# A two-direction delta-rule scan taken in lockstep over two head pairs, with its triangular inversion cut into three queued pieces

## The chip, the core and the metric

One core of one Trainium2 chip runs the whole kernel. The metric is the device time of one execution in microseconds (us), the median of three runs; lower is better.

The core has five instruction queues that run side by side and each keep their own order: TensorE (PE in the profile, with its weight loads as PEld), VectorE (DVE), ScalarE (ACT), GpSimd (POOL) and SyncE (SP, which here only issues DMAs; ACT and POOL issue some too). An instruction waits until the semaphores it needs are set, and everything behind it on its queue waits with it.

## The reference

One layer of a hybrid backbone: 1024 latent tokens and 256 context tokens, width 1024. The token mixer has three branches (neighbourhood attention, RWKV-7 time mixing, gMLP gating), then comes a SwiGLU network. The change is in the RWKV branch, a recurrence over the tokens in both directions, for 8 heads of width 64:

```python
def delta_scan(state0, inputs, emit):
    def step(S, inp):
        r_t, w_t, k_t, v_t, kk_t, a_t = inp
        s_kk = jnp.einsum('...vk,...k->...v', S, kk_t)
        S = (S * w_t[..., None, :] - s_kk[..., :, None] * (kk_t * a_t)[..., None, :]
             + v_t[..., :, None] * k_t[..., None, :])
        return S, (jnp.einsum('...vk,...k->...v', S, r_t) if emit else None)
    return lax.scan(step, state0, inputs)
...
state_ctx, ys_c = delta_scan(state0, scan_c, ctx_out)     # 256 context tokens, no output kept
_, ys_l = delta_scan(state_ctx, scan_l, True)             # 1024 latent tokens
```

The state S is 64 x 64 per head and direction. The backward direction runs over the flipped sequence.

## The kernel before

**The stages.** `phase0a` projects the inputs (to about 500 us of the span), `rwkv_run` does the scan, `attention` and `readout` follow, then the branch merge (`mixer`) and the SwiGLU network. A scheduling layer decides each engine's order: the code is written in the order of priority, and the layer puts an instruction on its queue where, by its own estimate of times, its inputs and buffers are there. So independent work that the code names later can stand earlier. The most important such work is the *fill*: 28 projections of 48 TensorE products each (128x512, `mm`, lines L216 to L218) that `fill(4)` and `fill(24)` ask for after the scan and after the attention, and that in fact stand in the gaps of the scan and of what follows. Each fill projection loads one 512 KB weight block, which ACT and POOL split in two halves.

**The scan.** The sequence is cut into chunks of 64 tokens, so that a step is a few 64-wide products instead of 64 token steps. A *head pair* (two heads, 128 partitions) is one of j = 0..3. A *job* is (j, i): 256 tokens of one head pair, both directions d = 0, 1; i = 0 is the context, i = 1..4 the latent tokens. The list `L` has 20 jobs, and neighbours in it alternate between two head pairs, so that job m + 2 goes on where job m ends. A job has these parts:

- `values`: loads the values (tile `rv`).
- `prep`: loads the keys, decays and so on (`kkl`, `li`, `kd`, `bb`, `rl`), makes `BK` (L635 to L638) and `KKe`, `KKo` (L640, L641) on DVE, the products into PSUM tiles `gr` on PE (L651, L652, transposes L655), and masks them on DVE into `G` (L662, L663), `BB` (L665, L666) and the halves of `KKe`, `KKo` (L669, L670); ACT copies the transposes (L678).
- `invert`: the inverse of (I + G), a 64 x 64 triangle for each chunk, head and direction. `G` goes to memory (`gs`, L687), comes back re-ordered as 16 x 16 diagonal blocks (`gz`, L689), and 15 elimination rounds on DVE (L697, L699: one multiply and one add each) and a transposed copy (L700) invert these. The result goes to memory and back (`ds`, L702; `Dc`, L704). Then for each direction the blocks are put together: `Db`, `Dt` (L713, DVE), products (L718, PE), `ET` (L720, DVE), and three rounds of products (L727, PE) and adds into `X` (L730, DVE). These products use one PSUM bank, tile `ho`.
- `step`, four times for each direction, chunk after chunk: `sc` products (L739, L740), a copy `ru` (L742, DVE), products with `X` (L744), a negated copy `ub` in two halves (L748 ACT, L749 DVE), the output products (L750 to L752), and the new state, which stands in one half of `rv`, in two halves (L763 DVE, L764 ACT); for latent jobs the result is copied to `y` (L768, ACT).

In the code, job m's steps are followed by the whole of `prep` and `invert` of job m + 2. PSUM tile `gr` has three banks, `ho` one, `sc` two, and the fill's `d` two.

Of the kernel before, what the change touches and what calls it, by code (L numbers as in the profile page):

```python
# [15 lines left out]
P = 128  # L16
# [40 lines left out]
class Kern:  # L57
# [7 lines left out]
    def build(self):  # L65
# [21 lines left out]
        self.nd, self.ngr = 2, 3  # L87
# [467 lines left out]
    def rwkv_run(self):  # L555
# [14 lines left out]
        for i in range(4):  # L570
            ub = rp.tile([P, P], F32, name=f"ub{i}")
            nc.gpsimd.memset(ub, 0.0)
            self.ub.append(ub)
        L = [(2 * g + j, i) for g in range(2) for i in range(5) for j in range(2)]
        rvs, Js = {}, {}

        def values(m):
            j, i = L[m]
            rv = rvs[m] = [[self.T([P, 4, 64], f"rv{d}{h}", 3) for h in range(2)] for d in range(2)]
            for d in range(2):  # L580
                if i == 0:
                    nc.gpsimd.memset(rv[d][0][0:64, 3 * d, :], 0.0)
                    nc.gpsimd.memset(rv[d][1][64:128, 3 * d, :], 0.0)
                V = s["vtok"][j]
                n0 = self.start(d, i)
                for h in range(2):
                    nc.sync.dma_start(rv[d][h][64 * (1 - h):64 * (1 - h) + 64, 0:4, :],
                                      bass.AP(V.tensor, V.offset + 64 * h + n0 * P, [[P, 64], [P * 64, 4], [1, 64]]))

        def prepare(m):  # L590
            j, i = L[m]
            Js[m] = [self.prep(m, j, d, i) for d in range(2)]
            self.invert(Js[m])
# [3 lines left out]
        values(0)  # L597
        prepare(1)
        values(1)
        for m, (j, i) in enumerate(L):  # L600
            if m + 2 < len(L):
                values(m + 2)
            y = [self.T([P, 2, P], f"y{d}", 2) for d in range(2)] if i else [None, None]
# [3 lines left out]
            if i:  # L607
                for d in range(2):
                    c0 = 4 * (i - 1) if d == 0 else 16 - 4 * i
                    nc.scalar.dma_start(s["Y"][d][j][:, 64 * c0:64 * c0 + 256], y[d].rearrange("p c v -> p (c v)"))  # L610
            if m + 2 < len(L):
                prepare(m + 2)

    def start(self, d, i):
        return 0 if i == 0 else (CT + 256 * (i - 1) if d == 0 else NT - 256 * i)

    def prep(self, m, j, d, i):
        nc, c, s = self.nc, self.c, self.s
        lat = i > 0
        n0 = self.start(d, i)  # L620
        kk, li, kd, bb = (self.T([P, 256], n, 2) for n in ("kkl", "li", "kd", "bb"))
        for t, x in ((li, s["li"][d]), (kk, s["kk"]), (kd, s["kd"][d]), (bb, s["bb"][d])):
            nc.sync.dma_start(t, x[j][:, n0:n0 + 256])
        if lat:
            r = self.T([P, 256], "rl", 2)
            nc.sync.dma_start(r, s["r"][j][:, n0 - CT:n0 - CT + 256])
        R = rev if d else (lambda x: x)
        E = self.T([P, 4, 65], "E", 6)
        nc.gpsimd.memset(E[:, :, 0:1], 1.0)
        nc.scalar.activation(E[:, :, 1:65], units(R(li)), AF.Exp, scale=-C05)  # L630
        le = self.T([P, 256], "le", 2)
        nc.scalar.activation(le, R(li), AF.Exp, scale=C05)
        BK = self.T([P, 4, P], "BK", 2)
        if d:
            nc.vector.tensor_tensor(BK[:, :, 64:128], units(kd)[:, ::-1, :], units(le)[:, :, ::-1], ALU.mult)  # L635
        else:
            nc.vector.tensor_tensor(BK[:, :, 64:128], units(kd), units(le), ALU.mult)
        nc.vector.scalar_tensor_tensor(BK[:, :, 0:64], units(R(bb)), 0.5, units(le), ALU.mult, ALU.mult)  # L638
        KKe, KKo = self.sets[(m % 3) * 2 + d]
        nc.vector.tensor_tensor(KKe[0:64, :, 0:64], E[0:64, :, 0:64], units(R(kk))[0:64], ALU.mult)  # L640
        nc.vector.tensor_tensor(KKo[64:128, :, 0:64], E[64:128, :, 0:64], units(R(kk))[64:128], ALU.mult)  # L641
        if lat:
            ee, rr = (E[:, :, 1:65], units(r)) if d == 0 else (E[:, :, 64:0:-1], units(r)[:, ::-1, :])
# [37 lines left out]
    def invert(self, jobs):  # L681
# [7 lines left out]
        nc.sync.dma_start(z, bass.AP(gs.tensor, gs.offset, [[1040, 64], [64, 16], [1, 16]]))  # L689
        DD, tmp = self.T([64, 2, 16, 16], "DD", 1), self.T([64, 64], "dtmp", 1)  # L690
# [13 lines left out]
        nc.sync.dma_start(Dc, bass.AP(ds.tensor, ds.offset, [[16, P], [2048, 16], [1, 16]]))  # L704
        bmb = c["bm"].rearrange("p (b t) -> p b t", t=16).unsqueeze(1).to_broadcast([P, 4, 4, 16])
# [4 lines left out]
        for d, J in enumerate(jobs):  # L710
# [4 lines left out]
            e = self.ps.tile([P, 4, 64], F32, name="ho", tag="ho", bufs=1)  # L715
# [6 lines left out]
            for t0 in (16, 32, 48):  # L722
                n = 64 - t0
                e = self.ps.tile([P, 4, n], F32, name="ho", tag="ho", bufs=1)
                for u in range(4):
                    for z in (0, 64):
                        nc.tensor.matmul(e[z:z + n, u, :], ET[z:z + 64, u, 0:n], src[z:z + 64, u, t0:64],  # L727
                                         start=True, stop=True)
                for z in (0, 64):
                    nc.vector.tensor_tensor(X[z:z + n, :, t0:64], e[z:z + n], Dt[z:z + n, :, t0:64], ALU.add)  # L730
# [3 lines left out]
    def step(self, J, d, i, u, rv, rvn, y):  # L734
        nc = self.nc
        lat, KKe, KKo, BB, X, E = J["lat"], J["KKe"], J["KKo"], J["BB"], J["X"], J["E"]
        v, w = (u, u + 1) if d == 0 else (3 - u, 2 - u)
        sc = self.ps.tile([P, 512], F32, name="sc", tag="sc", bufs=2)
# [683 lines left out]
```

## Time and profile before

| what | value |
|---|---|
| runs | 2453.37, 2454.89, 2456.29 us (median 2454.89) |
| the profiled execution | 2465.17 us, span 2463.4 us |
| mean granted TensorE clock | 0.97 |
| busy over the span | PE 96%, PEld 75%, DVE 67%, ACT 37%, POOL 28% |
| first and last `X` product of a step (L744) | 566.2 and 1218.7 us |
| first attention score product (L844) | 1248.5 us |

How to read the rows that follow. A row of the windows view gives a stretch of the span, then for each engine the busy time and the number of instructions in it, the granted TensorE clock (1.00 is full), the share of the DMA engines and their rate. A row of the groups view gives line, engine, operation, tiles written and read, shapes, the count, then the busy time in us and the mean of one in ns, then the idle time of the engine just before them and what ended it. A row of the timeline gives start and duration in us; what stands in square brackets is the engine's idle time before it and what ended that. TensorE runs an fp32 product in two passes, each of which is an instruction in the trace. Rows with a q behind the engine (SPq, ACTq) are the issue of a DMA.

### The profile page before, as it was taken

To read this page: it belongs to the slowest core of one execution; us is meant where nothing else is said; L and a number is where in the kernel's file an instruction comes from. 1 tells how busy PE (TensorE), PEld (TensorE's weight loads), DVE (VectorE), ACT (ScalarE), POOL (GpSimd) and SP (SyncE) were. 2 spreads that over 40 slices of the span, in tenths; PEclk is the share of its full clock that TensorE was granted. 3 is DMA by queue.
4 is the path that set the end of the run, shared out by engine and by line. 5 is a ranking of instruction groups with operands and counts; after the bars stand their busy time and mean duration, and the time that the engine had idled before them with its cause. 6 is when DMAs were issued, how large, how long until landed. Compare 5 with 4: busy or idle time off the path is not lost.

```text
span 2463.4 us, 39381 instructions
## 1 busy us (share of the span) xinstructions
PE 2353.5 (96%) x14520; PEld 1850.6 (75%) x14520; DVE 1639.5 (67%) x3496; ACT 914.1 (37%) x1845; POOL 684.3 (28%) x716
## 2 busy tenths in 40 slices
PE   6999999999999999999999999999699999999997
PEld 4778888876777776777777778778588888887886
DVE  8874446357776878688367873778676666655835
ACT  4432334232343443344345552232433333333321
POOL 6221213441211111211131231242533333325302
PEclk9999999999898999899999999999799999999999
DMA  7676434553343443332277547555132222237441
GB/s 252 208 231 168 140 124 154 175 164 80 99 99 77 109 100 90 98 100 69 69 204 196 169 151 272 175 188 167 60 98 83 77 78 86 91 109 279 162 171 52
DMA packets 275973, 336.92 MB, mean 137 GB/s; under 512 B 123298, under 2 KB 194210, under 8 KB 275780
## 3 DMA queue, kind: packets, MB, share of 16 engines
q1 hardware_dynamic: 208660, 240.39, 32.5%
q10 hardware_dynamic: 54608, 51.40, 6.8%
q0 software_dynamic: 12512, 42.62, 5.1%
q8 instruction: 115, 1.88, 0.3%
q14 instruction: 78, 0.64, 0.1%
HBM read 248.32 MB, written 85.99 MB: 136 GB/s over the span
## 4 chain that ended last, share of the span: by engine, by line
PE 67%; DVE 8%; issue 2%; DMA 2%; ACT 2%; POOL 1%; SPq 0%; DVEq 0%; ACTq 0%; POOLq 0%
PE d L217 12%; PE d L218 11%; PE d L216 11%; PE d L1008 3%; PE d L1009 3%; PE d L1007 3%; PE pv L892 3%; PE ho L727 2%; PE gr L652 2%; PE sc L744 2%; PE gr L651 1%; PE pt L878 1%; PE sc L739 1%; PE sc L752 1%; PE sc L750 1%
## 5 line engine op out<-in xcount | busy, mean ns | idle before, releaser
L217 PE MATMUL d<-hl,wh 128*128 128x512 f32 x1056 | 436.4, 413 | 0.0
L218 PE MATMUL d<-hh,wl 128*128 128x512 f32 x1056 | 433.8, 411 | 0.0
L216 PE MATMUL d<-hh,wh 128*128 128x512 f32 x1056 | 433.3, 410 | 0.0
L216 PEld LDWEIGHTS d<-hh,wh 128*128 128x128 f32 x1056 | 202.1, 191 | 42.2 <-issue 1.8
L218 PEld LDWEIGHTS d<-hh,wl 128*128 128x128 f32 x1056 | 201.7, 191 | 42.3 <-issue 2.0
L217 PEld LDWEIGHTS d<-hl,wh 128*128 128x128 f32 x1056 | 201.9, 191 | 41.9 <-issue 0.7
L208 DVE TENSOR_TENSOR wl<-wr,wh 128x1024 fp32r<-128x1024 f32 x51 | 64.9, 1273 | 159.6 <-ACT wh L204 111.2
L204 ACT ACTIVATE wh<-wr 128x1024 fp32r<-128x1024 f32 x79 | 83.5, 1057 | 196.9 <-PE d L217 161.1
L208 POOL TENSOR_TENSOR wl<-wr,wh 128x256 fp32r<-128x256 f32 x112 | 85.7, 797 | 248.3 <-ACT wh L204 194.4
L230 ACT ACTIVATE o<-wr 128x1024 fp32r<-128x1024 f32 (+1 forms) x64 | 59.0, 926 | 164.8 <-PE d L217 132.8
L233 DVE TENSOR_TENSOR o<-wr,o 128x1024 fp32r<-128x1024 f32 (+1 forms) x64 | 89.6, 1403 | 21.5 <-ACT o L230 21.1
L1008 PE MATMUL d<-dl,ah 128*128 128x512 f32 x252 | 98.7, 392 | 2.2 <-DVE dl L233 2.2
L764 ACT ACTIVATE rv<-sc,E 64x64 f32<-64x64 f32 x152 | 46.6, 308 | 142.6 <-DVE rv L763 133.5
L1009 PE MATMUL d<-dh,al 128*128 128x512 f32 x252 | 98.8, 392 | 0.0
L1007 PE MATMUL d<-dh,ah 128*128 128x512 f32 x252 | 98.7, 392 | 0.0
L233 DVE TENSOR_TENSOR al<-ar,ah 128x512 fp32r<-128x512 f32 x42 | 40.5, 979 | 78.5 <-ACT ah L230 78.5
L892 PE MATMUL pv<-pT,V 128*64 128x128 f32 (+2 forms) x640 | 91.2, 282 | 0.0
L1002 POOL TENSOR_TENSOR wl<-wr,wh 128x1024 fp32r<-128x1024 f32 x16 | 42.6, 2665 | 169.3 <-ACT wh L1001 125.8
L730 DVE TENSOR_TENSOR X<-ho,Dt 48x192 f32<-48x192 f32 (+2 forms) x240 | 68.3, 285 | 29.8 <-PE ho L727 24.8
L233 POOL TENSOR_TENSOR wl<-wr,wh 128x1024 fp32r<-128x1024 f32 x24 | 59.8, 2491 | 79.8 <-ACT wh L230 79.8
L892 PEld LDWEIGHTS pv<-pT,V 128*64 128x64 f32 (+2 forms) x640 | 68.3, 137 | 16.2 <-issue 10.3
L763 DVE TENSOR_SCALAR rv<-sc,E 64x64 f32<-64x64 f32 x152 | 41.8, 275 | 52.6 <-PE sc L752 35.9
(399 smaller groups left out, 6132.2 us busy)
## 6 DMA issues: line engine op xcount, KB each, us to landing
wr<-wgu SPq DMA_DIRECT2D x44, 512.0 KB
dr<-wdn SPq DMA_DIRECT2D x42, 512.0 KB
wa<-wada SPq DMA_DIRECT2D x32, 512.0 KB
wr<-win SPq DMA_DIRECT2D x31, 512.0 KB
wr<-win ACTq DMA_DIRECT2D x28, 512.0 KB
s_gt<-stg ACTq DMA_DIRECT2D x48, 256.0 KB
wr<-wbr SPq DMA_DIRECT2D x24, 512.0 KB
g<-s_gt SPq DMA_DIRECT2D x48, 256.0 KB
```

The lines of the kernel that those rows point to most:

```text
L204: nc.scalar.activation(hi[:, :n], raw[:, :n], AF.Copy)
L208: (lo_eng or self.lo_eng).tensor_tensor(lo[:, q], raw[:, q], hi[:, q].bitcast(F32), ALU.subtract)
L216: nc.tensor.matmul(ps, w, xh, start=first and k == 0, stop=False)
L217: nc.tensor.matmul(ps, w, xl, start=False, stop=False)
L218: self.last = nc.tensor.matmul(ps, lo[:, P * k:P * k + P], xh, start=False, stop=last and k == n - 1)
L230: nc.scalar.activation(hi, src, AF.Copy)
L233: (lo_eng or nc.vector).tensor_tensor(lo, src, hi.bitcast(F32), ALU.subtract)
L730: nc.vector.tensor_tensor(X[z:z + n, :, t0:64], e[z:z + n], Dt[z:z + n, :, t0:64], ALU.add)
L892: nc.tensor.matmul(o, V[0:k, vt, 64 * e:64 * e + 64], pt[0:k, i, :], start=(i == 0), stop=(i == len(cols) - 1))
L1007: nc.tensor.matmul(ps, xh, wh, start=first, stop=False)
L1008: nc.tensor.matmul(ps, xh, wl, start=False, stop=False)
L1009: nc.tensor.matmul(ps, xl, wh, start=False, stop=last)
```

## The change

The scan's jobs become 128 tokens of *two* head pairs: `L` has (g, i) with g = 0, 1 and i = 0..9 (i = 0, 1 is the context). There are still 20 jobs, the two groups alternate, and job m + 2 goes on where m ends. Tiles keep their sizes: the four chunk places of a tile are now two head pairs times two chunks. A job has two steps instead of four, and each does both head pairs at once: `step_in` (the products that need only the old state, in two PSUM tiles `sa` and `sb` of two banks each), `step_solve` and `step_out`. All step products are now 64 columns of weights wide (L750 and L751 become four products instead of two, L752 becomes two instead of one). The negated copy is done by ACT alone, the new state by DVE alone. Loads are issued once for each head pair, so each has half the size and there are twice as many; the backward direction reads its tiles in flipped order instead of loading other places.

`invert` is cut into `pivots` (to the load of `gz`), `substitute` (the elimination, to the load of `Dc`) and `blocks` (the rest). In the code they stand at three places: `blocks(m+1)` and `prepare(m+2)` behind the first step of job m, `substitute(m+2)` behind its second. `issue_after` keeps `blocks` behind the output products and the state update of the first step, and `substitute` behind the state update of the second. In `blocks` all products write 64 partitions, so that each `X` add is one instruction instead of two. `gr` has two banks instead of three, and the products of `blocks` now use the banks of `gr` too.

```diff
-        self.nd, self.ngr = 2, 3
+        self.nd, self.ngr = 2, 2
...
-        L = [(2 * g + j, i) for g in range(2) for i in range(5) for j in range(2)]
+        L = [(g, i) for i in range(10) for g in range(2)]
...
         def prepare(m):
-            j, i = L[m]
-            Js[m] = [self.prep(m, j, d, i) for d in range(2)]
-            self.invert(Js[m])
+            g, i = L[m]
+            Js[m] = [self.prep(m, g, d, i) for d in range(2)]
+            zs[m] = self.pivots(Js[m])
...
-            for u in range(4):
+            for uu in range(2):
+                st = [self.step_in(Js[m][d], d, uu, rvs[m][d]) for d in range(2)]
+                ub = [self.step_solve(Js[m][d], *st[d]) for d in range(2)]
                 for d in range(2):
-                    self.step(Js[m][d], d, i, u, rvs[m][d], rvs[m + 2][d] if i < 4 else None, y[d])
+                    self.step_out(Js[m][d], d, uu, ub[d], st[d], rvs[m][d], None if i == 9 else rvs[m + 2][d], y[d])
+                if uu == 0 and m + 1 < len(L):
+                    with self.tc.issue_after(self.out.ins), self.tc.issue_after(self.upd.ins):
+                        blocks(m + 1)
+                    if m + 2 < len(L):
+                        prepare(m + 2)
...
             if m + 2 < len(L):
-                prepare(m + 2)
+                with self.tc.issue_after(self.upd.ins):
+                    substitute(m + 2)
...
-            e = self.ps.tile([P, 4, 64], F32, name="ho", tag="ho", bufs=1)
+            e = self.ps.tile([P, 4, 64], F32, name="ho", tag="gr", bufs=self.ngr)
...
-                for z in (0, 64):
-                    nc.vector.tensor_tensor(X[z:z + n, :, t0:64], e[z:z + n], Dt[z:z + n, :, t0:64], ALU.add)
+                nc.vector.tensor_tensor(X[:, :, t0:64], e, Dt[:, :, t0:64], ALU.add)
...
-        nc.vector.tensor_copy(ru, sc[:, 0:64])
+        nc.vector.tensor_copy(ru, sa[:, :, 0:64])
...
+            nc.scalar.activation(ub[z:z + 64, :, z:z + 64], sa[z:z + 64, :, 64:128], AF.Copy, scale=-1.0)
...
+                self.upd = nc.vector.tensor_tensor(n[z][q, w::2, :], sb[q, :, q], E[q, tt::2, 64:65].to_broadcast([64, 2, 64]), ALU.mult)
```

**How the order moves on DVE.** The rows below are in DVE's order of the kernel before, in the middle of the scan. `dtmp` and `DD` are the elimination of one job, `Db`, `Dt`, `ET` and `X` the blocks of another, `G` and the `gr` reads the preparation of a third.

```order
L699 TENSOR_TENSOR DD<-DD,dtmp 64x11x5
L713 TENSOR_TENSOR Db<-Dc,c_bm 128x256
L713 TENSOR_TENSOR Dt<-Dc,c_bm 128x256 x2
L697 TENSOR_TENSOR dtmp<-gz,DD 64x60
L637 TENSOR_TENSOR BK<-kd,le 128x4x64
L720 TENSOR_TENSOR ET<-ho,c_om 128x256
L713 TENSOR_TENSOR Db<-Dc,c_bm 128x256
L699 TENSOR_TENSOR DD<-DD,dtmp 64x10x6
L662 TENSOR_TENSOR G<-gr,c_gmask 64x256
L697 TENSOR_TENSOR dtmp<-gz,DD 64x63
L730 TENSOR_TENSOR X<-ho,Dt 48x4x48 x2
```

The three pieces there belong to three jobs and are mixed. The same place on DVE in the changed kernel, from the last elimination round (now L721, L723) on; `Db` is now L741, `ET` L748, `X` L756, the state update L804, `G` L682 and L683:

```order
L721 TENSOR_TENSOR dtmp<-gz,DD 64x15
L723 TENSOR_TENSOR DD<-DD,dtmp 64x15
L724 COPY DD<-DD 64x256
L741 TENSOR_TENSOR Db<-Dc,c_bm 128x256
L741 TENSOR_TENSOR Dt<-Dc,c_bm 128x256 x2
L748 TENSOR_TENSOR ET<-ho,c_om 128x256
L741 TENSOR_TENSOR Db<-Dc,c_bm 128x256
```

Three `X` adds of the first direction follow, and then, still on DVE:

```order
L748 TENSOR_TENSOR ET<-ho,c_om 128x256
L756 TENSOR_TENSOR X<-ho,Dt 128x4x48
L804 TENSOR_TENSOR rv_6212<-sb,E 64x2x64
L804 TENSOR_TENSOR rv_6213<-sb,E 64x2x64
L756 TENSOR_TENSOR X<-ho,Dt 128x4x32
L756 TENSOR_TENSOR X<-ho,Dt 128x4x16
L682 TENSOR_TENSOR G<-gr,c_gmask 64x256
L683 TENSOR_TENSOR G<-gr,c_gmask 64x256
```

Now `Db` stands directly behind the copy whose result comes to it by way of memory, and `G` of the next job stands behind the last `X`. In the repeating pattern the elimination of the next job, which reads that `G` by way of memory, follows behind the steps.

**How the fill moves on PE.** Behind the last output product of the scan stood, in the kernel before, 120 fill products, then the attention; of the 1344 fill products about 900 stood within the scan.

```order
L751 MATMUL sc<-rv_10939,KKo_3989 128x64
L752 MATMUL sc<-ub_4000,BB 128x128
L216 MATMUL d<-hh_404,wh 128x512
L217 MATMUL d<-hl_405,wh 128x512
L218 MATMUL d<-hh_404,wl 128x512
```

In the changed kernel the attention's first products (L883) stand there. Some 87 fill products stand in each of the jobs 1 to 13 (before: about 40 in each of all jobs), the last of them in the fifteenth job of twenty, and about 55 of the 87 in one stretch ahead of the first `blocks` product (L746).

```order
L774 MATMUL sb<-rv_10847,KKo_3989 64x64 x2
L784 MATMUL sa<-ru,X 64x64 x4
L799 MATMUL sb<-ub_4000,BB 64x128 x4
L883 MATMUL SA<-K_11869,Q_11870 128x264
L883 MATMUL SB<-K_11869,Q_11870 128x256
```

So the scan now holds all of the fill, and nothing of it is left for the gap at its end and for the attention.

More of the change, by code (lines that the diff above doesn't have):

```diff
@@ L679, in prep, with pivots @@
         return dict(KKe=KKe, KKo=KKo, G=G, BB=BB, E=E, n0=n0, lat=lat)
-    def invert(self, jobs):
+    def pivots(self, jobs):
         nc, c = self.nc, self.c
@@ L704, in invert, with blocks @@
         nc.sync.dma_start(Dc, bass.AP(ds.tensor, ds.offset, [[16, P], [2048, 16], [1, 16]]))
+        return Dc
+    def blocks(self, jobs, Dc):
+        nc, c = self.nc, self.c
         bmb = c["bm"].rearrange("p (b t) -> p b t", t=16).unsqueeze(1).to_broadcast([P, 4, 4, 16])
@@ new lines, in step_in @@
+        tt = uu if d == 0 else 1 - uu
+        sa = self.ps.tile([P, 2, 256], F32, name="sa", tag="sa", bufs=2)
+        sb = self.ps.tile([P, 2, 256], F32, name="sb", tag="sb", bufs=2)
+        halves = (slice(0, 64), slice(64, 128))
+        kk = J["KKe"], J["KKo"]
+        for jj in range(2):
+            for z, q in enumerate(halves):
+                nc.tensor.matmul(sa[q, jj, 0:64], kk[z][:, 2 * jj + tt, 0:64], rv[z][:, 2 * jj + tt, :], start=True, stop=True)
+        for jj in range(2):
+            for z in range(2):
+                for h, q in enumerate(halves):
+                    if J["lat"] or h == z:
+                        nc.tensor.matmul(sb[q, jj, 64 * z:64 * z + 64], kk[z][:, 2 * jj + tt, 64 + 64 * h:128 + 64 * h],
+                                         rv[z][:, 2 * jj + tt, :], start=(jj == 0 and (z == 0 or not J["lat"])), stop=False)
@@ new lines, in step_out @@
+    def step_out(self, J, d, uu, ub, st, rv, rvn, y):
+        nc = self.nc
+        tt, _, sb = st
+        BB, E = J["BB"], J["E"]
+        for jj in range(2):
+            for h in (0, 64):
+                q = slice(h, h + 64)
+                c = slice(0, P) if J["lat"] else q
+                self.out = nc.tensor.matmul(sb[q, jj, c], BB[:, 2 * jj + tt, q], ub[:, jj, c], start=False, stop=(jj == 1))
+        if uu == 0 or rvn is not None:
+            n, w = (rv, 1 - tt) if uu == 0 else (rvn, d)
+            for z in range(2):
+                q = slice(64 * z, 64 * z + 64)
+                self.upd = nc.vector.tensor_tensor(n[z][q, w::2, :], sb[q, :, q], E[q, tt::2, 64:65].to_broadcast([64, 2, 64]), ALU.mult)
+        if J["lat"]:
+            for z, p0 in ((0, 64), (1, 0)):
+                nc.scalar.activation(y[64 * tt:64 * tt + 64, :, 64 * z:64 * z + 64], sb[p0:p0 + 64, :, 64 * z:64 * z + 64], AF.Copy)
```

123 lines of the change are left out of this document (56 added, 67 removed).

## The prediction

> **What bounds the kernel now.** I read the page's busy shares first, then the windows by stage, the groups of the scan, the start times of one line, and last the timeline of single jobs.
>
> ```profile
> PE 2353.5 (96%) x14520; PEld 1850.6 (75%) x14520; DVE 1639.5 (67%) x3496; ACT 914.1 (37%) x1845; POOL 684.3 (28%) x716
> 566.00:1221.00 655.00, 644.14 (x6224) 467.87 (x6224) 486.40 (x1696) 256.01 (x863) 109.12 (x216) 0.95 0.35 89
> 1221.00:1248.00 27.00, 26.97 (x118) 21.78 (x116) 1.49 (x1) 6.70 (x9) 5.81 (x9) 1.00 0.67 198
> 1248.00:1485.00 237.00, 225.91 (x1476) 178.48 (x1477) 188.02 (x576) 129.11 (x245) 63.66 (x39) 0.99 0.62 180
> 1485.00:1525.00 40.00, 40.00 (x177) 32.93 (x176) 10.98 (x14) 10.82 (x15) 3.38 (x5) 1.00 0.79 275
> ```
>
> PE is the bound in every stage: 98% of the scan's 655 us, all of the 27 us gap to the attention, 95% of the attention. What fills it is seen when L216, one third of the fill, is asked for alone:
>
> ```profile
> 566.00:1221.00 655.00, 120.55 (x268) 0.95 0.35 89
> 1248.00:1485.00 237.00, 20.12 (x50) 0.99 0.62 180
> 1494.74 0.39 PE L217 MATMUL d<-hl,wh 128*128 128x512 f32 x1
> 1494.97 0.39 PE L218 MATMUL d<-hh,wl 128*128 128x512 f32 x1
> L744 PE MATMUL sc<-ru,X x640: 218/218/367, 566.2 to 1218.7; 64*64 64x64 f32 x160
> ```
>
> A fill product costs PE 0.23 us where they stand in a row (1494.74 to 1494.97). The scan holds 3 x 268 = 804 of them, 185 us; so the scan's own products take 655 - 185 = 470 us, 23.5 us for each of 20 jobs. From the first to the last step (79 of 80 places) the scan takes 652.5 us: a job every 33.0 us. Its chain of waits is not the bound, because several jobs are under way at once. In these rows `G` of a later job is made between two `X` adds:
>
> ```profile
> 1108.24 0.57 DVE L730 TENSOR_TENSOR X<-ho,Dt 32x128 f32<-32x128 f32 x2
> 1109.09 0.42 DVE L663 TENSOR_TENSOR G<-gr,c_gmask 64x256 f32<-64x256 f32 x1
> 1109.68 0.46 DVE L730 TENSOR_TENSOR X<-ho,Dt 16x64 f32<-16x64 f32 x2
> ```
>
> **The change, part by part.** *Steps.* Half as many, each twice as wide:
>
> ```profile
> L742 DVE COPY ru<-sc 128x64 f32<-128x64 f32 x160 | 35.1, 222 | 34.8 <-PE sc L740 32.1
> L763 DVE TENSOR_SCALAR rv<-sc,E 64x64 f32<-64x64 f32 x152 | 41.8, 275 | 52.6 <-PE sc L752 35.9 <-PE sc L759 12.4 <-ACT rv L764 1.6
> L749 DVE TENSOR_SCALAR ub<-sc 64x64 f32<-64x64 f32 x128 | 28.6, 227 | 22.1 <-ACT ub L748 18.8
> L768 ACT ACTIVATE y<-sc 64x64 f32<-64x64 f32 x256 | 54.9, 215 | 12.6 <-PE sc L752 9.2 <-DVE KKo L641 1.0
> ```
>
> Two chunks of one direction cost DVE 2 x (222 + 275 + 227) = 1448 ns. Now it is one `ru` and two updates of 128 columns, about 300 ns each (L742 and L763 with some 70 ns for 64 more columns): 0.55 us less, 80 times, 44 us. ACT saves about as much by its own merged copies. Neither engine is the bound, so this counts nothing by itself. On PE two 64-wide products take the place of one 128-wide one, and both pairs of a step stand together; I take PE's own work as 3 us less per job (20.5 us), between 0 and 5.
>
> *DMAs.* SP issues some 31 instead of 17 per job, about 0.6 us each (L689 below): 18 us of a job, hidden unless `gz` or `ds` stands behind one that waits: 0 to 2 us per job, taken within the first term below.
>
> *The inversion in three pieces.* DVE's order above has lost the overlap. `G` of job m+1 stands behind the last `X` of job m, the elimination of m+1 behind the steps, and `Db` directly behind its copy. The banks ask for the same: `prep` takes its three `gr` tiles for each direction from the two banks that `blocks` has just used. So each job's whole chain lies end to end: `G`, memory, elimination, memory, blocks, products, next `G`. Its pieces, from jobs late in the scan:
>
> ```profile
> 1090.53 0.42 DVE L663 TENSOR_TENSOR G<-gr,c_gmask 64x256 f32<-64x256 f32 x1
> 1091.38 0.58 ACTq L687 DMA_DIRECT2D gs<-G  x1
> 1094.51 0.58 SPq L689 DMA_DIRECT2D gz<-gs  x1
> 1098.43 0.16 DVE L697 TENSOR_TENSOR dtmp<-gz,DD 64x15 f32<-64x15 f32 x1
> 1156.94 0.36 DVE L700 COPY DD<-DD 64x256 f32<-64x256 f32 x1
> 1157.36 0.59 SPq L702 DMA_DIRECT2D ds<-DD  x1
> 1160.50 0.38 SPq L704 DMA_DIRECT2D Dc<-ds  x1
> 1163.66 0.42 DVE L713 TENSOR_TENSOR Db<-Dc,c_bm 128x256 f32<-128x256 f32 x1 [0.60 <-DMA Dc<-ds]
> 1189.65 0.42 DVE L713 TENSOR_TENSOR Db<-Dc,c_bm 128x256 f32<-128x256 f32 x1
> 1200.41 0.74 DVE L730 TENSOR_TENSOR X<-ho,Dt 48x192 f32<-48x192 f32 x2 [0.82 <-PE ho L727]
> 1203.76 0.47 DVE L730 TENSOR_TENSOR X<-ho,Dt 16x64 f32<-16x64 f32 x2 [0.51 <-PE ho L727]
> 573.15 0.46 DVE L730 TENSOR_TENSOR X<-ho,Dt 16x64 f32<-16x64 f32 x2 [0.21 <-PE ho L727]
> L699 DVE TENSOR_TENSOR DD<-DD,dtmp 64x15 f32<-64x15 f32 (+2 forms) x300 | 71.2, 237 | 5.3
> L697 DVE TENSOR_TENSOR dtmp<-gz,DD 64x15 f32<-64x15 f32 (+2 forms) x300 | 68.5, 228 | 10.0 <-POOL DD L693 4.1 <-DMA gz<-gs 0.3
> L700 DVE COPY DD<-DD 64x256 f32<-64x256 f32 x20 | 7.3, 367 | 0.2
> L640 DVE TENSOR_TENSOR KKe<-E,kkl 64x256 f32<-64x256 f32 x40 | 21.5, 539 | 10.3 <-ACT E L630 10.0 <-issue 0.2
> L662 DVE TENSOR_TENSOR G<-gr,c_gmask 64x256 f32<-64x256 f32 x40 | 16.5, 412 | 5.3 <-PE gr L652 4.1 <-PE gr L651 0.7
> L669 DVE TENSOR_TENSOR KKe<-gr,c_gmask 64x512 f32<-64x512 f32 x32 | 22.2, 695 | 0.9
> L678 ACT ACTIVATE KKe<-gr 64x256 f32<-64x256 f32 x40 | 15.1, 378 | 0.5
> ```
>
> 1. From `G` (ends 1090.95) to the first multiply (1098.43): 7.5 us. This is the shortest of the twenty, whose first multiplies often had DVE to wait for; with longer SP queues I take 8.4, bounds 7.5 and 9.6. The steps' tail on DVE lies beside it.
> 2. Elimination: (71.2 + 68.5) / 20 = 7.0 us, the copy 0.37, and about 1.4 for `KKe`, `KKo` between (L640): 8.8, bounds 8.0 and 10.
> 3. Copy (ends 1157.30) to `Db` (1163.66, DVE waited for the DMA): 6.4 us; in the last job, from the copy at 1182.6 to 1189.65, 7.1. With more traffic 7.5, bounds 6.4 and 10.
> 4. Blocks of both directions: 1189.65 to 1204.23 is 14.6 us, DVE waiting for PE between. One `X` add instead of two saves about 0.3 six times, the second bank about 1: 12.0, bounds 9.9 (nothing of the fill ahead of the rounds) and 14.5.
> 5. Last `X` to the second direction's `G`: products 1.6 and 1.2, transposes 0.9 (estimates from 16, 8 and 8 PE instructions of about 0.1 us), masks 4 x 0.42 + 0.70 = 2.4 (L662, L669), four ACT copies 1.5 (L678), `G` 0.42: 8.0, bounds 6.7 and 9.
>
> The sum is 44.7 us a job; the bounds add to 38.5 and 53. PE needs 20.5 + 87 x 0.23 = 40.5 us in a job that holds fill, less than 44.7, so the loop decides. The first `X` is done at 573.6 (573.15 + 0.46), taken as before, since the chain to it is the same. The last job's `X` comes 19 periods later, 849.3 us, less 1.5 us for each of three context periods with fewer masks; its two steps take 6 us. The scan ends at 573.6 + 849.3 - 4.5 + 6 = 1424.4 instead of 1220.5: +203.9 us.
>
> *After the scan.* What opens the attention:
>
> ```profile
> 1216.85 0.37 SPq L793 DMA_DIRECT2D V<-s_vatok  x1
> L844 PE MATMUL SA<-K,Q x64: 281/387/448, 1248.5 to 1462.6; 128*128 128x264 f32 x16, 128*128 128x352 f32 x16, 128*128 128x288 f32 x16, 128*128 128x384 f32 x16
> ```
>
> Its loads start with the scan's end (1216.85) and its first product comes at 1248.5. The gap of 27 us keeps its length, and PE, which had fill there, idles in it. The attention loses 3 x 50 products, 34.5 us, in a stretch where PE was 95% and DVE 79% (188.02 of 237) busy; I take two thirds, 23 us, between 0 and 34.5. Behind it the run of fill is 111 products shorter (399 to 288, counted in the order, of which the mixer's are the rest): 25.5 us, less about 6 (a guess: load, split and first product of a weight block) that the mixer's start then shows: 19.5. Together -42.5 us, between -20 and -60.
>
> The sum is +161 us. Against the profiled execution's 2465.2 this gives 2626; that execution was 10.3 us over the median 2454.9, so the forecast is **2616 us**.
>
> **A rule on the DMAs.** Terms 1 and 3 are two dependent DMAs each, and the rows give 6.4 us at the least where DVE waited. The Trainium skill, "DMA: Bandwidth & Descriptors", in its cost components, puts one DMA at a fixed 2.0 us and bytes over 436 GB/s; two would take about 4.5 us here (estimate), the loop would be 38 us long and the time that of rival A below. The trace disagrees: 6.4 and 7.5 us at the least, for small strided pieces.
>
> **Rivals.** *A short loop (rival A).* All pieces at their lower bounds, 38.5 us. Then PE decides where there is fill: 13 x 40.5 + 6 x 38.5 = 757.5 instead of 849.3, the scan ends 92 us earlier, 2524. For it: the rows of before are from a DVE shared by three jobs. Against it: term 4's rounds still have fill products between them on PE.
>
> *A slow clock (rival B).* From job 15 on no fill is left, and PE idles through terms 2 and 3, some 16 us.
>
> ```profile
> 700.00:800.00 100.00, 97.14 (x844) 72.46 (x845) 73.68 (x248) 39.46 (x134) 16.18 (x31) 0.88 0.35 88
> 1754.00:1792.00 38.00, 20.78 (x71) 14.34 (x72) 31.78 (x34) 21.36 (x34) 18.07 (x12) 0.51 0.14 50
> ```
>
> Where PE was 55% busy (38 us from 1754) the clock was 0.51. PE's part of terms 4 and 5 is some 8 us at full clock; doubled in six jobs it is +47 us, 2663, and in half of the others too, +98, 2714. The Trainium skill, "TensorE: Matmul & The Clock Gate", on how the gate bites in real kernels, asks for no PE gaps over some 3.4 us and would have it so in every job. By that rule the time is 2663 or more; the trace agrees only in part, for at 700 to 800 the clock fell to 0.88 with PE 97% busy.
>
> *Faster (rival C).* The loop hides: if the elimination and both trips to memory overlap with the blocks of the job ahead, terms 1 to 3 drop out of the period, PE decides, and 13 x 40.5 + 6 x 20.5 = 650 against 627 (19 x 33.0) gives +23 in the scan and, with -42.5 behind it, 2435. It decides below a mean period of 35.2 us (33.0 + 42.5 / 19). For it: nothing in the code ties `prepare(m+2)` to `blocks(m+1)`. Against it: DVE's order, and the banks.
>
> **How the numbers follow.** The forecast (2560 to 2680) has 0.55, A (2490 to 2560) 0.20, B (2680 and above) 0.15, C 0.07, and 0.03 lies between A and C. The range, 2520 to 2715, leaves out C, the low end of A and the worst of B. Some 0.2% (5 us) is what a measurement of this kernel can tell from no change. Faster by more 0.07, within it 0.02, slower 0.91.
>
> **What would show it.** Step 1 to 5: starts of the `Db` line (L741) some 45 us apart, and rows in which DVE waits for `Dc` and `gz`. The scan's end: last L799 near 1424. The fill: PE's busy share about 90% up to the fifteenth job, then below 60%, with the clock near half. After it: PE idle for about 25 us ahead of the first L883, an attention of some 215 us. I am wrong if `Db` comes every 35 us, or if `G` of job m+1 starts before the last `X` of job m.

## The result, and the profile after

The changed kernel takes 2721.9 us (median of 4 runs, 2716.3 to 2743.1) where the kernel before takes 2455.0: ratio 1.110, 95% interval 1.105 to 1.114. The forecast was slower, 2616 us, range 2520 to 2715: the sign holds, and so does the loop that it names; the time is 106 us over the forecast and 7 us over the range. The profiled execution took 2721.4 us (span 2719.6), 256 us more than that of before.

The page's busy line and clock line:

```profile
PE 2414.2 (89%) x15352; PEld 1924.5 (71%) x15352; DVE 1605.2 (59%) x3168; ACT 866.2 (32%) x1565; POOL 683.6 (25%) x708
PEclk9999999967899989787666788899989999999999
```

The windows by stage, columns as before:

```profile
566.00:1231.00 665.00, 609.70 (x5517) 465.82 (x5515) 340.36 (x994) 174.33 (x454) 112.33 (x197) 0.85 0.33 85
1231.00:1482.00 251.00, 145.93 (x1930) 122.00 (x1926) 129.22 (x416) 51.65 (x165) 15.44 (x34) 0.66 0.19 42
1482.00:1500.00 18.00, 0.61 (x8) 0.37 (x8) 1.56 (x2) 2.80 (x4) 0.57 (x2) 0.59 0.67 175
1500.00:1740.00 240.00, 215.04 (x1288) 166.88 (x1288) 178.87 (x568) 119.53 (x229) 49.06 (x23) 0.87 0.53 151
```

The lines of the step's `X` product (now L784) and of the attention's first products (now L883): shortest, median and longest in ns, first and last start in us:

```profile
L784 PE MATMUL sa<-ru,X x640: 218/267/366, 566.0 to 1481.1; 64*64 64x64 f32 x160
L883 PE MATMUL SA<-K,Q x64: 282/407/689, 1500.0 to 1726.4; 128*128 128x264 f32 x16, 128*128 128x352 f32 x16, 128*128 128x288 f32 x16, 128*128 128x384 f32 x16
```

The first stretch is the scan with fill, the second the scan without: PE is 58% busy there (145.93 of 251) at a clock of 0.66. In the gap PE does nothing, and in the attention, where the fill is missing, the clock is 0.87 instead of 0.99. It stands at half from 1485.3, in the gap, through the first 19 us of the attention:

```profile
1485.30:1519.40 34.10, 18.24 (x65) 13.65 (x66) 16.12 (x42) 8.09 (x15) 4.82 (x2) 0.50 0.83 223
```

The same boundaries in both kernels:

| stretch | before | after | forecast | measured |
|---|---|---|---|---|
| start to the last `X` product of a step | 1218.7 | 1481.1 | +203.9 | +262.4 |
| from there to the first score product | 29.8 | 18.9 | 0 | -10.9 |
| first to last score product | 214.1 | 226.4 | -23 | +12.3 |
| from there to the end of the span | 1000.8 | 993.2 | -19.5 | -7.6 |
| sum | | | +161.4 | +256.2 |

So 58 us of the miss are in the scan, and 36 us are a gain behind it that did not come. The other 11 us are not in the stages: the forecast took off 10.3 us because the profiled execution of before lay that far above its median, while that of the changed kernel lies at its own (2721.4 and 2721.9).

That the chain lies end to end is shown by two stretches of DVE's timeline, one job with fill and one without. Each runs from the elimination's copy through `Db`, the last `X`, the last `G` and the first multiply to the next copy:

```profile
943.47 0.38 DVE L724 COPY DD<-DD 64x256 f32<-64x256 f32 x1
949.49 0.60 DVE L741 TENSOR_TENSOR Db<-Dc,c_bm 128x256 f32<-128x256 f32 x1 [5.64 <-DMA Dc<-ds]
967.85 0.23 DVE L756 TENSOR_TENSOR X<-ho,Dt 128x64 f32<-128x64 f32 x1 [2.22 <-PE ho L755]
977.67 0.42 DVE L683 TENSOR_TENSOR G<-gr,c_gmask 64x256 f32<-64x256 f32 x1
985.38 0.60 DVE L721 TENSOR_TENSOR dtmp<-gz,DD 64x15 f32<-64x15 f32 x1
997.45 0.37 DVE L724 COPY DD<-DD 64x256 f32<-64x256 f32 x1
...
1286.61 0.37 DVE L724 COPY DD<-DD 64x256 f32<-64x256 f32 x1
1292.39 0.43 DVE L741 TENSOR_TENSOR Db<-Dc,c_bm 128x256 f32<-128x256 f32 x1 [5.41 <-DMA Dc<-ds]
1304.87 0.22 DVE L756 TENSOR_TENSOR X<-ho,Dt 128x64 f32<-128x64 f32 x1 [0.68 <-PE ho L755]
1313.86 0.42 DVE L683 TENSOR_TENSOR G<-gr,c_gmask 64x256 f32<-64x256 f32 x1
1321.52 0.65 DVE L721 TENSOR_TENSOR dtmp<-gz,DD 64x15 f32<-64x15 f32 x1
1330.94 0.37 DVE L724 COPY DD<-DD 64x256 f32<-64x256 f32 x1
```

The windows of the two stretches:

```profile
943.85:997.82 53.97, 48.75 (x414) 37.54 (x413) 26.47 (x75) 13.35 (x36) 9.52 (x16) 0.78 0.33 85
1286.98:1331.40 44.42, 25.02 (x328) 20.95 (x328) 24.38 (x75) 9.55 (x30) 3.84 (x8) 0.65 0.24 55
```

And the group of `Db`, with the idle time of DVE just before it at the end, in the kernel before and in the changed one:

```profile
L713 DVE TENSOR_TENSOR Db<-Dc,c_bm 128x256 f32<-128x256 f32 x40 | 19.1, 478 | 4.2 <-DMA Dc<-ds 4.1
L741 DVE TENSOR_TENSOR Db<-Dc,c_bm 128x256 f32<-128x256 f32 x40 | 17.1, 428 | 117.9 <-DMA Dc<-ds 117.9
```

`G` stands behind the last `X` in both, and DVE waits for the memory trip of `Dc` with nothing else to do: 117.9 us over 20 jobs, 5.9 us each, where it waited 4.2 us in all before. The job with fill takes 54.0 us, the one without 44.4; what differs most are the blocks, 949.49 to 968.08 (18.6 us) against 1292.39 to 1305.09 (12.7). The job with fill that is shown is one of the long ones: in jobs 4 to 13 the blocks take 12.5 to 18.6 us, 14.7 in the mean. PE's timeline between the rounds of the first shows why:

```profile
950.14 1.12 PE L746 MATMUL ho<-Db,G 64*64 64x64 f32 x16 [5.10 <-DVE Db L741]
951.19 0.79 PE L217 MATMUL d<-hl,wh 128*128 128x512 f32 x1
951.78 0.63 PE L218 MATMUL d<-hh,wl 128*128 128x512 f32 x1
952.21 0.63 PE L216 MATMUL d<-hh,wh 128*128 128x512 f32 x1
952.77 1.09 PE L755 MATMUL ho<-Dt,ET 64*64 64x48 f32 x16
```

After 5.10 us of idle PE the three fill products ahead of the next round take 952.77 - 951.19 = 1.58 us, 0.53 each, where 0.23 was their price in the row of before. The round waits behind them. The window of that stretch has PE busy almost throughout, at half its clock:

```profile
949.41:973.31 23.90, 23.17 (x208) 17.60 (x209) 8.10 (x21) 2.38 (x8) 0.39 (x1) 0.50 0.11 29
```

The Trainium skill, "TensorE: Matmul & The Clock Gate", in the part on how the gate bites in real kernels, has a wait of more than some 3.4 us in every turn of a loop start each turn cold; this trace agrees, with an idle stretch of 5.1 us ahead of this half-clock one, and mean clocks of 0.78 and 0.65 in the two jobs shown.

### The profile page after: what moved, and what is told of

Read it like the earlier page. It is cut to its first block, busy times and chain, and to the rows that moved or that the text cites. A ratio compares the mean times of both kernels' runs of the same rounds, so it can differ in the third digit from the quotient of the medians.

```text
span 2719.6 us, 40780 instructions
## 1 busy us (share of the span) xinstructions
PE 2414.2 (89%) x15352; PEld 1924.5 (71%) x15352; DVE 1605.2 (59%) x3168; ACT 866.2 (32%) x1565; POOL 683.6 (25%) x708
## 3 DMA queue, kind: packets, MB, share of 16 engines
q1 hardware_dynamic: 237588, 240.40, 29.8%
## 5 line engine op out<-in xcount | busy, mean ns | idle before, releaser
L746 PE MATMUL ho<-Db,G 64*64 64x64 f32 x640 | 40.5, 296 | 144.4 <-DVE Db L741 144.4
L746 PEld LDWEIGHTS ho<-Db,G 64*64 64x64 f32 x640 | 34.5, 201 | 151.5 <-DVE Db L741 151.5
L756 DVE TENSOR_TENSOR X<-ho,Dt 128x192 f32<-128x192 f32 (+2 forms) x120 | 35.0, 291 | 161.8 <-PE ho L755 159.9
L788 ACT ACTIVATE ub<-sa 64x128 f32<-64x128 f32 x160 | 43.4, 271 | 254.5 <-PE sa L784 186.7
L931 PE MATMUL pv<-pT,V 128*64 128x128 f32 (+2 forms) x640 | 100.1, 297 | 6.0 <-ACT ot L933 3.6
```

The costliest lines, as they stand in the source:

```text
L746: nc.tensor.matmul(e[z:z + 64, u, :], J["G"][z:z + 64, u, :], Db[z:z + 64, u, :], start=True, stop=True)
L931: nc.tensor.matmul(o, V[0:k, vt, 64 * e:64 * e + 64], pt[0:k, i, :], start=(i == 0), stop=(i == len(cols) - 1))
```

## Experiments

Theory 1 is that the shared PSUM banks lay the chain end to end: `gr` tiles of `prep` and `blocks` go round the same banks in the order of the code, so the products of `prepare(m+2)` wait until `blocks(m+1)`, which waits for memory, is done with them. Its rival, theory 2, is that the three places in the code and the `issue_after` waits make the loop. Theory 3 is on the fill: it is worth less behind the scan than its products cost, because PE's clock falls where they are missing, and it lengthens the loop where it is. Theories 4 and 5 came with the runs. The kernel before ran at 2457 to 2460 us beside them.

### A bank of its own for the blocks

```diff
-        self.nd, self.ngr = 2, 2
+        self.nd, self.ngr = 1, 2
...
-            e = self.ps.tile([P, 4, 64], F32, name="ho", tag="gr", bufs=self.ngr)
+            e = self.ps.tile([P, 4, 64], F32, name="ho", tag="ho", bufs=1)
```

> The changed kernel with one edit: the products of the blocks get a PSUM bank of their own again, taken from the fill (which then has one bank instead of two). Theory 1 (the shared banks tie the preparation of the next job behind the blocks, and so lay each job's chain end to end): the masked products G of the next job are again made between the X adds, the period falls from 47.4 us to what TensorE needs, some 20.5 us of its own work and the fill that stands there, 26 to 32 us; the scan ends near 1100 to 1180 instead of 1482, some 300 fill products more stand behind it, and the time is 2400 to 2480. Theory 2 (the places where the code queues the pieces, and the waits that hold them behind the steps, make the loop): the banks change little, the period stays above 44 us and the time above 2650.

2498.9 us, ratio to before 1.018 (1.014 to 1.022): 223 us of the 267 are gone. Its `Db` group:

```profile
L741 DVE TENSOR_TENSOR Db<-Dc,c_bm 128x256 f32<-128x256 f32 x40 | 17.0, 425 | 4.0 <-DMA Dc<-ds 3.9
```

The step's `X` product and the blocks' first product:

```profile
L784 PE MATMUL sa<-ru,X x640: 218/218/366, 568.3 to 1128.9; 64*64 64x64 f32 x160
L746 PE MATMUL ho<-Db,G x640: 218/218/366, 561.9 to 1119.0; 64*64 64x64 f32 x160
```

A piece of DVE's timeline:

```profile
811.04 0.41 DVE L741 TENSOR_TENSOR Db<-Dc,c_bm 128x256 f32<-128x256 f32 x1
811.49 0.41 DVE L682 TENSOR_TENSOR G<-gr,c_gmask 64x256 f32<-64x256 f32 x1
812.52 0.36 DVE L756 TENSOR_TENSOR X<-ho,Dt 128x192 f32<-128x192 f32 x1 [0.62 <-PE ho L755]
813.03 0.42 DVE L683 TENSOR_TENSOR G<-gr,c_gmask 64x256 f32<-64x256 f32 x1
```

`G` of the next job stands between the `X` adds again, the wait for `Dc` is 4.0 us in all, and the scan ends at 1128.9, 352 us earlier than in the changed kernel and 90 us earlier than before. The places and waits are untouched, so theory 2 does not hold. The time is still 19 us above what theory 1 expected; more on that below.

### The kernel before, with its banks shared

```diff
-        self.nd, self.ngr = 2, 3
+        self.nd, self.ngr = 2, 2
...
-            e = self.ps.tile([P, 4, 64], F32, name="ho", tag="ho", bufs=1)
+            e = self.ps.tile([P, 4, 64], F32, name="ho", tag="gr", bufs=self.ngr)
```

> The kernel before with one part of the change alone: the products of the blocks use the two banks of the preparation (two instead of three, none of their own); jobs, steps and the inversion in one piece stay. Theory 1: this alone makes the loop serial; its period is the five pieces with the old pairs of X adds and four steps instead of two, 50 to 58 us instead of 33, the scan ends near 1540 to 1650 instead of 1220, the time is 2720 to 2850. Theory 2: the old queueing keeps two jobs in flight whatever the banks, the time stays under 2520.

2835.8 us, ratio 1.154 (1.150 to 1.160). The one edit does to the kernel before what the whole change did, and more. (It also leaves two banks unused; the next run tells the number of banks from their sharing.) Its `Db` group and its step's `X` product:

```profile
L713 DVE TENSOR_TENSOR Db<-Dc,c_bm 128x256 f32<-128x256 f32 x40 | 18.4, 460 | 120.6 <-DMA Dc<-ds 120.6
```

```profile
L744 PE MATMUL sc<-ru,X x640: 218/267/367, 571.1 to 1598.8; 64*64 64x64 f32 x160
```

### Three banks, still shared

```diff
-        self.nd, self.ngr = 2, 2
+        self.nd, self.ngr = 1, 3
```

> The changed kernel with three banks for gr instead of two, the products of blocks still in the same banks; the third bank is taken from the fill, as in the run with a bank of its own for blocks. It is the control for that run: the same number of banks, another division. Theory 1 (sharing): the tiles still go round the same banks in the order of the code, so the preparation's products still wait for the blocks of the job before; period 44 to 49 us, last X product of a step at 1420 to 1500 us, time 2680 to 2780 us (the fill's single bank may cost some 30 us). Rival (the number of banks, or the fill's single bank, is what shortened the period there): period 28 to 34 us, time below 2580 us.

2699.4 us, ratio 1.098 (1.093 to 1.102). As many banks as in the first experiment, but the loop stays, as the same two views show:

```profile
L741 DVE TENSOR_TENSOR Db<-Dc,c_bm 128x256 f32<-128x256 f32 x40 | 17.4, 436 | 117.4 <-DMA Dc<-ds 117.4
```

```profile
L784 PE MATMUL sa<-ru,X x640: 217/252/367, 567.7 to 1462.5; 64*64 64x64 f32 x160
```

So it is not the number of banks but that the two stages take turns in them. The Trainium skill, "Perfetto Trace Analysis", in its optimization strategy, says that the same gap repeated on the engine that should be saturated can mean too little SBUF or PSUM for the next tile. The place is right here (PSUM), but one more buffer alone does little: a third bank took 23 us off, a division of the banks 223.

### The changed kernel without its waits

```diff
-                    with self.tc.issue_after(self.out.ins), self.tc.issue_after(self.upd.ins):
-                        blocks(m + 1)
+                    blocks(m + 1)
...
-                with self.tc.issue_after(self.upd.ins):
-                    substitute(m + 2)
+                substitute(m + 2)
```

> The changed kernel without its two issue_after waits; banks as in the changed kernel. Theory 1 (shared banks): the chain stays end to end, G of the next job behind the last X, period 46 to 49 us, time 2690 to 2760 us. Theory 2 (the queued places and their waits): the pieces overlap again, period below 38 us, time below 2600 us.

2729.7 us, one run, as theory 1 had it. The last step's `X` product stands at 1499.4, and the wait for `Dc` is that of the changed kernel:

```profile
L739 DVE TENSOR_TENSOR Db<-Dc,c_bm 128x256 f32<-128x256 f32 x40 | 17.1, 426 | 119.5 <-DMA Dc<-ds 119.5
```

With shared banks the waits make no difference that this run can tell.

### Eight projections held behind the scan

```diff
-        for _ in range(n):
-            next(self.filler, None)
+        for i in range(n):
+            if n == 24 and i >= 16:
+                with self.tc.issue_after(self.out.ins):
+                    next(self.filler, None)
+            else:
+                next(self.filler, None)
```

> The changed kernel with the last 8 fill projections (384 products, 88 us of TensorE) held behind the scan's last product. Theory 3 (without fill the gap and the attention lose the clock, which ate the gain forecast there; and fill lengthens the scan's period from 43.0 to 48.5 us): the fill ends five jobs earlier, so the scan shortens by 5 x 5.5 = 27 us; the attention's clock returns from 0.87 to about 0.98, it and the gap take the fill nearly free, and the time from the scan's end to the mixer's first products is 278 to 300 us as against 278 now: 2690 to 2720. Rival (the clock does not matter there, TensorE's sum counts): 88 us of products come on top behind the scan and 27 are saved in it, some 2750 to 2785.

2734.7 us (2725.0 to 2750.8), between the two expectations. Of the profiled execution (span 2749.0, at the upper end) the step's products, and the attention's:

```profile
L788 PE MATMUL sa<-ru,X x640: 218/311/366, 567.7 to 1491.1; 64*64 64x64 f32 x160
L887 PE MATMUL SA<-K,Q x64: 281/398/448, 1520.9 to 1732.0; 128*128 128x264 f32 x16, 128*128 128x352 f32 x16, 128*128 128x288 f32 x16, 128*128 128x384 f32 x16
```

Some 232 of the 384 held products (53 us of PE at 0.23 each) stand in the gap and the attention. The gap is 29.8 us instead of 18.9, the attention 211.1 instead of 226.4: the stretch with 53 us more work in it is 4 us shorter. The rest, some 152 products or 35 us, stand behind the attention, where the span has 1017.0 us left instead of 993.2.

The scan ends 10 us later, where 27 us less were expected. Jobs 10 to 13, now without fill, fell from 50.3 to 46.0 us in the mean; but jobs 1 to 9, with nearly the same fill in both kernels, took 51.7 us here and 49.0 in the changed kernel. What a single profiled execution says of a job with fill is thus uncertain by some 3 us.

### The kernel before, with eight projections left out

```diff
-        self.fill(24)
+        self.fill(16)
```

The last eight gate projections aren't computed; one branch reads the gates of another.

> The kernel before with the last 8 of the 28 fill projections left out (the gates of one branch are read from another one's, so the output is not the reference's): no fill is left for the gap and the attention. Theory 3: the scan stays as it is, the attention's clock falls from 0.99 to about 0.87 and its 237 us stay within 10 us of that; only the 111 products behind it (25 us) are saved: 2425 to 2440. Rival (TensorE's sum counts): all 384 products are saved, 88 us, less the gap of 27 us: 2385 to 2400.

2450.3 us, ratio 0.997 (0.994 to 1.000). 384 products, 88 us of PE, are gone, and the time falls by 10 us. That is above both expectations, and far from the rival's. Its step's and attention's products:

```profile
L744 PE MATMUL sc<-ru,X x640: 218/218/367, 568.9 to 1210.8; 64*64 64x64 f32 x160
L844 PE MATMUL SA<-K,Q x64: 283/406/686, 1229.4 to 1454.8; 128*128 128x264 f32 x16, 128*128 128x352 f32 x16, 128*128 128x288 f32 x16, 128*128 128x384 f32 x16
```

The windows of its gap and attention:

```profile
1211.00:1229.00 18.00, 0.98 (x8) 0.74 (x6) 1.43 (x2) 2.90 (x5) 0.57 (x2) 0.60 0.69 179
1229.00:1465.00 236.00, 212.02 (x1278) 166.82 (x1279) 177.45 (x567) 119.69 (x229) 47.93 (x22) 0.86 0.54 153
```

Gap and attention read as in the changed kernel (18.6 and 225.4 us, clock 0.86), though the scan is that of before. What the fill's absence does there is thus no matter of the scan. Behind the attention 9 us are saved (991.4 us from the last score product to the end, before 1000.8), where theory 3 had expected 25.

### All gate projections held behind the scan

The same edit with `i >= 0` instead of `i >= 16`.

> The changed kernel with all 24 gate projections held behind the scan's last output product, so that the scan runs with next to no fill; nothing is left out. Theory 3a (fill products between the loop's own products cost 5.5 us a job, as jobs 4 to 13 at 48.5 us against jobs 14 to 19 at 43.0 us suggest): period 42 to 44 us in all jobs, last X product of a step near 1400 us, and the 1152 products come back behind it as 265 us less some 50 us that the gap and the attention hide: about 2850 us (2820 to 2880). Rival (the fill costs the loop nothing, the last jobs are shorter for want of a preparation): period 47 to 49 us in jobs 4 to 13, time above 2900 us. A second rival (a slower clock without the fill makes every piece longer): period above 50 us, time above 2950 us.

2856.7 us, one run, in the time that theory 3a expected, though its price for the fill was too high, as the period shows. A window of its scan without fill:

```profile
1000.00:1200.00 200.00, 109.35 (x1450) 91.97 (x1452) 106.53 (x336) 40.07 (x126) 15.80 (x34) 0.64 0.24 53
```

The step's `X` product, the blocks' first product (here L750) and the attention's:

```profile
L788 PE MATMUL sa<-ru,X x640: 217/311/367, 567.9 to 1421.4; 64*64 64x64 f32 x160
L750 PE MATMUL ho<-Db,G x640: 218/312/367, 560.2 to 1409.6; 64*64 64x64 f32 x160
L887 PE MATMUL SA<-K,Q x64: 282/396/448, 1451.1 to 1663.1; 128*128 128x264 f32 x16, 128*128 128x352 f32 x16, 128*128 128x288 f32 x16, 128*128 128x384 f32 x16
```

Without fill the period is 44.3 us (last `X` adds end at 573.1 and 1415.5, 19 periods); in the changed kernel it is 47.4 (574.6 to 1475.1). By these two profiled executions fill costs the loop 3 us a job, 58 us in all: 8.4 us in each of jobs 1 to 3 (44.1 us in the mean without it, 52.5 with it), 3.4 in jobs 4 to 13 (45.2 and 48.5) and nothing in jobs 14 to 19 (43.1 and 43.0). The last jobs are 2 us shorter than the middle ones without any fill, so the 5.5 us of the theory were not all the fill's. All this holds although without fill the clock is lower (0.64) and the median of the blocks' first product is 312 ns, where the overlapped scan of the first experiment has 218. Gap and attention are 29.7 and 212.0 us long here, with some 232 fill products in them. With before and the two experiments above:

| kernel | fill products in gap and attention | gap, us | score products, first to last, us |
|---|---|---|---|
| before | 245 | 29.8 | 214.1 |
| all held | 232 | 29.7 | 212.0 |
| eight held | 232 | 29.8 | 211.1 |
| changed | 0 | 18.9 | 226.4 |
| before, eight left out | 0 | 18.6 | 225.4 |

In these five, 53 to 56 us of PE work (at 0.23 a product) change the two stretches by -4 to 0 us together. The profiles of the other kernels scatter more: with some 210 to 240 fill products the two stretches take 242.3 to 254.2 us together there, without any 237.4 to 241.8, and the score products alone 211.3 to 222.2 us with fill and 218.8 to 223.3 without. What holds in all of them is the attention's clock, 0.96 to 0.99 with fill and 0.86 to 0.89 without. So the fill costs little there; that the clock is the reason fits, but no run changed the clock alone. Why the gap is 11 us longer with the fill is not settled; nothing was run that separates the loads from it.

### One bank for both `sa` tiles

The bank for `blocks` now comes from the steps: both directions' `sa` tiles share one bank, and the fill has its two again. Against the first experiment:

```diff
-        self.nd, self.ngr = 1, 2
+        self.nd, self.ngr = 2, 2
...
-        sa = self.ps.tile([P, 2, 256], F32, name="sa", tag="sa", bufs=2)
+        if d == 0:
+            self.sa = self.ps.tile([P, 2, 2, P], F32, name="sa", tag="sa", bufs=1)
+        sa = self.sa[:, d]
```

> The run with a bank of its own for blocks, but with that bank taken from the steps instead of the fill: the sa tiles of both directions share one bank, and the fill keeps two. Theory 4 (what that run lost against the kernel before was the fill's single bank: 249 x 3 products in the 200 us from 1410 are 0.27 us each where 0.23 is their price, some 30 us, and PE idled 36 us in its scan): time 2430 to 2470 us, ratio to before 0.985 to 1.003, PE busy at least 96% in the scan. Rival (the loss is in the wider steps or in the longer gap ahead of the attention): 2485 to 2510 us. If the shared sa bank ties the two directions together, the period of 28.8 us grows, to 32 us or more, and the time is not below 2500 us.

2468.8 us, ratio 1.002 (0.999 to 1.005): no difference from before, and 30 us faster than the first experiment, as theory 4 expected. Of the first experiment, the window of the fill run behind the attention, for one third of the fill:

```profile
1410.00:1610.00 200.00, 100.12 (x249) 46.84 (x249) 0.99 0.44 148
```

The scan of this run:

```profile
566.00:1150.00 584.00, 554.61 (x6854) 411.89 (x6852) 415.01 (x1388) 198.06 (x572) 100.47 (x186) 0.92 0.40 95
```

```profile
L786 PE MATMUL sa<-ru,X x640: 217/219/366, 569.0 to 1148.5; 64*64 64x64 f32 x160
```

With a single bank the run's 747 products took 200 us, 28 more than at 0.23 each. In this run's scan PE is 95% busy, not the 96% expected, at a clock of 0.92. The scan is 70 us shorter than before and yet nothing is won: it holds 584 fill products instead of 803 (50 us that come later), and PE's own work is 554.6 - 584 x 0.23 = 420 us instead of 459 (an estimate, with every fill product at 0.23). Gap and attention are 8 us longer together than before, and what follows them 60.

### The wide step with the inversion in one piece

Against the last run: `prepare(m+2)`, `substitute(m+2)` and `blocks(m+2)` stand together behind the steps of job m, without waits.

> The run with one bank for both sa tiles, but the inversion not cut: prepare(m+2), substitute(m+2) and blocks(m+2) stand together behind the steps of job m, as in the kernel before, without waits; what is left of the change is the wide step. Theory 5 (with banks apart, three pieces or one make no difference, since PE is the bound and the order comes out mixed either way): ratio to before 0.993 to 1.008, first L885-like score product of the attention within 25 us of that run's 1178.6. Rival (the pieces help once the banks are apart): 1.01 or more, that is 2485 us or more. Rival (the pieces and their waits hurt): 0.99 or less, 2435 us or less.

2475.4 us, ratio 1.007 (1.004 to 1.010). It lies in theory 5's window; against the run before it is some 0.5% longer (1.007 to 1.002, with intervals that just meet), but that run has the waits as well. What the cut itself is worth is read from the next one.

### The pieces without waits

The last run but one without the two `issue_after` waits.

> The run with one bank for both sa tiles, the pieces where the change put them, but without the two issue_after waits. Theory 5 (waits without weight): ratio to before 0.993 to 1.008. Rival (the waits hold up work that could run): 0.99 or less, 2435 us or less.

2449.1 us, ratio 0.995 (0.992 to 0.998), inside theory 5's window: the one version that beats both kernels, 0.5% under before. The step's `X` product here, and in the run in one piece:

```profile
L784 PE MATMUL sa<-ru,X x640: 218/218/366, 573.3 to 1148.4; 64*64 64x64 f32 x160
L783 PE MATMUL sa<-ru,X x640: 218/218/367, 572.9 to 1167.0; 64*64 64x64 f32 x160
```

The scan is as long as with the waits (1148.5). What this run gains on that one in the profiled executions (spans 2446.4 and 2461.4) lies behind the scan, so the waits are not shown to be the cause. Against the run in one piece, which has no waits either, the cut is all that differs: 0.995 against 1.007, some 1%, with intervals well apart, and 19 of the 24 us between the two profiled executions are in the scan. So theory 5 does not hold for the cut: each ratio lies in its window, but with the banks apart the three pieces are worth about 1%.

## Why the prediction was right or wrong

*That the loop decides: right.* `G` always stands behind the last `X`, as forecast, and the banks are the cause: the prediction named DVE's order and the banks side by side, and the runs put it on the banks alone.

*The loop's terms: right without fill, too small with it.* The prediction priced the period at 44.7 us for all jobs. The means of the pieces, cut as in the two jobs shown:

| term | forecast | jobs 4 to 13 | jobs 14 to 19 | jobs 4 to 13, all fill held |
|---|---|---|---|---|
| 1. last `G` to the first multiply | 8.4 | 8.7 | 6.8 | 7.9 |
| 2. elimination | 8.8 | 10.3 | 9.1 | 9.5 |
| 3. copy to `Db` | 7.5 | 6.0 | 5.5 | 5.5 |
| 4. blocks | 12.0 | 14.7 | 12.7 | 12.6 |
| 5. last `X` to the last `G` | 8.0 | 8.9 | 8.9 | 9.5 |
| period | 44.7 | 48.5 | 43.0 | 45.2 |

Against the forecast of 844.8 us for 19 periods (849.3 less 4.5) stand 900.5: the ten jobs 4 to 13 give +38, jobs 14 to 19 give -10, and jobs 1 to 3 give +28 (55.1, 53.3 and 49.1 us; the prediction had made them shorter). The step that failed in the scan is the sentence that PE's 40.5 us fit into 44.7, by which the fill costs nothing there. With all gate projections held the 19 periods take 842.4 us (573.1 to 1415.5), 2 us from the forecast, and jobs 1 to 3 take 44.1 in the mean: the 58 us between the two are the fill's (products, loads and splits together), by one profiled execution of each kernel. PE needs 40.5 us at full clock; at the 0.85 granted in the scan with fill it is 47.6 (estimate), and the fill stands in front of the rounds, at 0.53 us a product in the job shown. Whether PE's sum at that clock or the place of the fill sets the price was not separated. Term 4 was the term to widen: its 14.7 lies just beyond the bound of 14.5.

That the sum comes so close without fill is in part luck. Term 3 was 2.0 us too long and term 1 0.5, terms 2, 4 and 5 were 0.7, 0.6 and 1.5 too short. In term 5, eight products of about 0.1 us had been entered as 1.2, not 0.8.

*PE's own work: right.* 3 us less per job were assumed, 0 to 5; 459 to 420 us in the run with one bank for both `sa` tiles is 2.0 per job.

*Longer DMA queues: right for most jobs.* In the mean, term 3 fell below its lower bound (5.5 to 6.0 where 6.4 was the bound), and term 1 is 0.3 over its price in jobs 4 to 13 and under it after them. In jobs 1, 2, 7 and 12 it is 11.3 to 11.5 us, above its bound of 9.6: there `gz` was issued 6 to 8 us after `G`, in most others 3. The price for a pair of DMAs worked out from the Trainium skill ("DMA: Bandwidth & Descriptors", cost components), some 4.5 us (estimate), is 1.0 to 1.5 under what term 3 measured; the page fits it to DMAs issued by GpSimd, while those of term 3 are issued by SP. The loop of 38 us that went with it did not come.

*After the scan: wrong.* -42.5 us was forecast, -6.2 measured. The failed step is "I take two thirds, 23 us": the attention's fill was priced as its products' time, while the window of before (95% busy, clock 0.99) was kept for an attention without it. In the runs the attention's clock falls to 0.86 to 0.89 where its fill is missing, and in the five kernels of the table it is 11 to 15 us longer, not 23 shorter. That the slower clock is what lengthens it fits but is not shown. That the gap keeps its 27 us was wrong too, by 11 us in the other direction, and of the 19.5 us behind the attention 7.6 came; why not more is open.

*The rivals.* B had the slow clock right (0.66 where it had put half), and its time (2663 to 2714) is the nearest, but its place was off, so the nearness is luck: in the jobs without fill the blocks were 0.7 us over their price and shorter terms 1 and 3 made up for it; the loss is in the jobs with fill and in the attention. A's loop of 38.5 us did not come. C is what the change does once the banks are apart: its price of 2435 us stands against 2499, 2469 and 2449 measured.

## What to carry to other kernels

When two stages share rotating PSUM buffers, as `prep` and `blocks` do here, each waits for the other in the order of the code: look whether a tile of the stage that waits for memory stands ahead of the next job's first product in the same rotation, and divide the banks rather than add one. Don't price filler products by their duration alone: here, in a stretch with small holes, they went with a higher clock and cost little, and in a loop with long holes they stood, slowed, in front of the loop's own products. A sum for PE has to be made at the clock that the loop will be granted.

## What the runs showed of the hardware that was not expected

- Without the 53 to 56 us of fill products in them, gap and attention (240 us) were 0 to 4 us longer, not shorter, in the five kernels compared: the attention's clock went from 0.99 to 0.86 with PE still 90% busy (212.02 of 236).
- Two dependent DMAs of small pieces, from the copy to `Db`, took 5.5 to 6.0 us in the mean where DVE waited for them, under the shortest read from the kernel before, 6.4.
- A 64x64 fp32 product has a median of 218 ns in the overlapped scan and 312 ns in the scan without fill, where the clock is 0.64.
- The clock stood at half, with PE 97% busy, over the 24 us of blocks and what followed them that came after 5.1 us of idle PE (23.17 of 23.90 us).
